# Gate matrices of a product-key expert layer: one-hot matrices built for eight tokens by two wide VectorE instructions, and gate matmuls that write the four tokens of a PSUM bank interleaved

## The chip, the cores and the metric

One Trainium2 chip, one core of it. The metric is the device time of one execution of the whole kernel in microseconds (us). The median of three runs of the kernel before is 1547.26 us (1546.43 to 1547.27).

## The reference, cut to what matters

The kernel computes two transformer-like blocks over 256 tokens of width 1024. The part that the change touches is in the first block, the PEER layer: per token and head (8 heads) it finds the 16 best of 128 x 128 product keys and weights those experts by a softmax.

```python
def peer(h, w_query, sub_keys, u_tab, v_tab):
    ...
    fv, fpos = lax.top_k(cand, P_TOPK)                 # 16 per head, 8 heads: 128 slots per token
    eidx = jnp.take_along_axis(cidx, fpos, axis=-1)    # expert = i1 * 128 + i2
    g = jax.nn.softmax(fv, axis=-1)
    u = u_tab[eidx]
    act = gelu(einsum('td,thkd->thk', xb, u))
    return einsum('thk,thkd->td', g * act, v_tab[eidx])
```

The kernel gathers nothing. It computes the activations of all 16384 experts densely (`peer_u`, 128 units of 128 experts), multiplies them by a gate that is zero where a token did not choose an expert, and multiplies the product by `peer_v`. The gate of one token is a 128 x 128 matrix: entry (i2, i1) is the sum of the weights g of the slots that chose that expert. With the 128 slots on the partitions it is one matmul of two one-hot matrices, one of them scaled by g.

## The kernel before, in words

`peer` has three stages that matter here. **Search** (lines 795 to 926) finds the experts, and `finish` leaves, for each slot (partition) and token, the two indices `ib[:, 0]` and `ib[:, 1]` and the weight. The weight is scaled by 32768 and split in two terms that are exact in fp16, `gp[:, 0]` and `gp[:, 1]`; all four are fp32 rows of 256 tokens. **Gate stage** (lines 928 to 965) builds the gate matrices. **Product stage** (from line 967) multiplies and streams `peer_v`.

The gate stage runs 32 groups of eight tokens (`OG` = 8). For a group, `onehots` issues on VectorE, per token, one `tensor_scalar` that compares a row 0..127 (`iob`, fp16) with the token's second index (`o`, line 941), and two that compare it with the first index and multiply by one half of the weight (`go`, line 943): 24 instructions of 128 elements. The loop calls `onehots(og + 1)` ahead of the matmuls of group og; `o` and `go` have two buffers. TensorE then does, per token, two accumulating matmuls of 128 columns, `o` stationary and `go` moving (line 958): 16 per group, four tokens side by side in each of two PSUM banks. ScalarE scales each bank into the staging tile `stg` (line 961), laid out as index, then 16 tokens, so that what it writes is one fp32 word in every 64 bytes. Every second group ScalarE's queue issues a 1 MB store of `stg` to the DRAM tensor `gd` (line 963).

Behind the gate matmuls of each group the loop puts one unit of `peer_u`, `U`: `fill` (lines 101 to 122) issues a 1 MB load on SP's queue for two units, casts one later unit on ScalarE (`whi`, line 112) and subtracts for another on VectorE (`wlo`, line 120), three to four units ahead of use; 24 matmuls of 256 columns follow (lines 163 to 165), then a Gelu on ScalarE (line 793). Order on each engine is program order. On VectorE a group is therefore 24 one-hot instructions and one `wlo`; on TensorE 16 gate matmuls and 24 matmuls of the unit; on ScalarE two `stg`, one `whi`, one Gelu.

Before the stage TensorE runs units alone, the last of them ending where the first gate matmul starts. Behind it seven units are left (`UKEEP`), and the product stage loads `gd` back (`gload`, line 979) once its last store has landed.

Of the kernel before, what the change touches and what calls it, by code (L numbers as in the profile page):

```python
# [13 lines left out]
F32 = mybir.dt.float32  # L14
F32R = mybir.dt.float32r
BF = mybir.dt.bfloat16
F16 = mybir.dt.float16
# [3 lines left out]
OP = mybir.AluOpType  # L21
# [4 lines left out]
T = 256  # L26
# [9 lines left out]
UKEEP = 7  # L36
TG = 16
OG = 8
GI = 8
LOADS = 9  # L40
SPLITS = 4
GSCALE = 32768.0
# [22 lines left out]
class Kx:  # L65
# [696 lines left out]
    def peer(self):  # L762
        nc, tc, a = self.nc, self.tc, self.a
# [4 lines left out]
        drp = ctx.enter_context(tc.tile_pool(name="pdr", bufs=1, space=DRAM))  # L768
        c1 = ExitStack()
        pz = c1.enter_context(tc.tile_pool(name="pz", bufs=1))  # L770
        gp = pz.tile([128, 2, T], F32, name="gp")
        ib = pz.tile([128, 2, T], F32, name="ib")
        acts = {}
        c2 = ExitStack()
        pk = c2.enter_context(tc.tile_pool(name="pk", bufs=1))
# [20 lines left out]
        with c2:  # L796
# [39 lines left out]
            for hd in range(1, 8):  # L836
# [5 lines left out]
                for i in range(2 if hd > 1 else 0):  # L842
                    p = self.unit("w_query", 2 * hd + i, h)
# [11 lines left out]
            pf_ = c2.enter_context(tc.tile_pool(name="pf", bufs=1))  # L855
# [4 lines left out]
            def finish():  # L860
                g = [pf_.tile([128, 8, 16], F32, name=f"g{tt}") for tt in range(2)]
                pf = [pf_.tile([128, 2, 8, 16], F32, name=f"pf{tt}") for tt in range(2)]
                sxf = [pf_.tile([128, 2, 8, 16], F32, name=f"sxf{tt}") for tt in range(2)]
                for tt in range(2):
                    v = fv[tt]
                    nc.vector.tensor_tensor(g[tt], v, v[:, :, 0:1].to_broadcast([128, 8, 16]), op=OP.subtract)
                    nc.scalar.activation(g[tt], g[tt], AF.Exp)
                for tt in range(2):
                    pi = pft.tile([128, 2, 8, 16], U32, name="pi")
                    nc.vector.tensor_scalar(pi[:, 0], fx[tt], 4, None, op0=OP.logical_shift_right)  # L870
                    nc.vector.tensor_scalar(pi[:, 1], fx[tt], 15, None, op0=OP.bitwise_and)
                    nc.vector.tensor_copy(sxf[tt].rearrange("p s h a -> p h s a"), sx[tt])
                    nc.vector.tensor_copy(pf[tt], pi)
                for tt in range(2):
                    gz = pft.tile([128, 8], F32, name="gz")
                    nc.vector.tensor_reduce(gz, g[tt], axis=AX.X, op=OP.add)
                    nc.vector.reciprocal(gz, gz)
                    nc.vector.tensor_tensor(g[tt], g[tt], gz[:, :, None].to_broadcast([128, 8, 16]), op=OP.mult)
                for _ in range(FW):
                    yield  # L880
                for tt in range(2):
                    p = self.side()
                    for j, src in enumerate((sxf[tt][:, 0], sxf[tt][:, 1], pf[tt][:, 0], pf[tt][:, 1])):
                        nc.tensor.transpose(p[:, j * 128:(j + 1) * 128], src.rearrange("p a b -> p (a b)"),
                                            self.ident)
                    ts = slice(tt * 128, (tt + 1) * 128)
                    p = p.rearrange("p (k s t) -> p k s t", k=2, s=2)
                    nc.scalar.copy(sxT[:, :, ts], p[:, 0])
                    nc.scalar.copy(posT[:, :, ts], p[:, 1])
                p = self.side()  # L890
                for tt in range(2):
                    nc.tensor.transpose(p[:, tt * 128:(tt + 1) * 128], g[tt].rearrange("p a b -> p (a b)"),
                                        self.ident)
                slot = pf_.tile([128, T], F32, name="slot")
                nc.scalar.mul(slot, p[:, :T], GSCALE)
                yield
                acc = self.bank(0)
                last = None
                for a0 in range(0, 16, FA):
                    cur = []  # L900
                    for a in range(a0, a0 + FA):
                        pb = self.side()
                        nc.tensor.matmul(pb, pick[:, a].rearrange("p h w -> p (h w)"),
                                         sxT.rearrange("p s t -> p (s t)"), start=True, stop=True)
                        t = pft.tile([128, 2 * T], BF, name="hit", bufs=2 * FA)
                        nc.vector.scalar_tensor_tensor(t, posT.rearrange("p s t -> p (s t)"), float(a), pb,
                                                       op0=OP.is_equal, op1=OP.mult)
                        cur.append((a, t))
                    yield
                    for a, t in cur:  # L910
                        nc.tensor.matmul(acc, identb, t, start=a == 0, stop=a == 15)
                nc.scalar.copy(ib, acc.rearrange("p (j t) -> p j t", j=2))
                g16 = pf_.tile([128, T], F16, name="g16")
                nc.vector.tensor_copy(g16, slot)
                nc.vector.tensor_copy(gp[:, 0], g16)
                nc.vector.tensor_tensor(gp[:, 1], slot, gp[:, 0], op=OP.subtract)

            self.side_cycle = ("s", "s", "a1", "a2")
            self.tasks.append(finish())
            while self.tasks:  # L920
                self.tick()
                if len(pre) > T // OG + UKEEP:
                    U(pre.popleft())
            while len(pre) > T // OG + UKEEP:
                U(pre.popleft())
            self.side_cycle = ("s",)

        with ExitStack() as c3:
            pg = c3.enter_context(tc.tile_pool(name="pg", bufs=1))
            pgt = c3.enter_context(tc.tile_pool(name="pgt", bufs=2))  # L930
            iob = pg.tile([128, 128], F16, name="iob")
            nc.gpsimd.iota(iob, pattern=[[1, 128]], base=0, channel_multiplier=0,
                           allow_small_or_imprecise_dtypes=True)
            stg = None

            def onehots(og):
                o = pgt.tile([128, OG, 128], F16, name="o")
                go = pgt.tile([128, OG, 2, 128], F16, name="go")
                for i in range(OG):
                    t = slice(og * OG + i, og * OG + i + 1)  # L940
                    nc.vector.tensor_scalar(o[:, i], iob, ib[:, 1, t], None, op0=OP.is_equal)  # L941
                    for j in range(2):
                        nc.vector.tensor_scalar(go[:, i, j], iob, ib[:, 0, t], gp[:, j, t],  # L943
                                                op0=OP.is_equal, op1=OP.mult)
                return o, go

            nxt = onehots(0)
            for og in range(T // OG):
                o2, go = nxt
                if og + 1 < T // OG:  # L950
                    nxt = onehots(og + 1)
                if og % (TG // OG) == 0:
                    stg = pgt.tile([128, 128, TG], F32, name="stg")
                for q in range(OG // 4):
                    p = self.side().rearrange("p (t i) -> p t i", t=4)
                    for i in range(4):
                        for j in range(2):
                            nc.tensor.matmul(p[:, i], o2[:, q * 4 + i], go[:, q * 4 + i, j],  # L958
                                             start=i == 0 and j == 0, stop=j == 1, skip_group_check=True)
                    e0 = (og % (TG // OG)) * OG + q * 4  # L960
                    nc.scalar.mul(stg[:, :, e0:e0 + 4].rearrange("p i t -> p t i"), p, 1.0 / GSCALE)
                if og % (TG // OG) == TG // OG - 1:
                    nc.scalar.dma_start(gd[:, og * OG // TG], stg)
                if len(pre) > UKEEP:
                    U(pre.popleft())
# [3 lines left out]
        with ExitStack() as c4:  # L969
# [5 lines left out]
            def gload(i):  # L975
                if i * GI < NB:
                    gts[i] = gt = pv.tile([128, 8 * (T + 2)], F32, name="gt")[:, :8 * T].rearrange(
                        "p (g e) -> p g e", g=T // TG)
                    (nc.gpsimd if i < 2 else nc.scalar).dma_start(gt, gd[:, :, i * GI:(i + 1) * GI].rearrange("p g i t -> p g (i t)"))

            wts = {}

            def w_mult(b):
                if b >= NB:
                    return
                t = acts[b]
                gv = gts[b // GI][:, :, (b % GI) * TG:(b % GI + 1) * TG]
                tv = t.rearrange("p (g t) -> p g t", t=TG)
                nc.vector.tensor_tensor(tv, tv, gv, op=OP.mult)  # L989
                if b % GI == GI - 1:  # L990
                    gload(b // GI + 2)

# [583 lines left out]
```

## Time and profile before

| | us |
|---|---|
| median of three runs | 1547.26 |
| the profiled execution | 1546.58 |
| its span in the trace | 1544.9 |
| first one-hot instruction | 379.89 |
| first matmul of the first unit in the gate stage | 384.93 |
| first matmul of the last unit in the gate stage | 570.04 |

Times in the views below count from the span's start. A row of a group of instructions gives the count, the busy time in us, the mean duration of one in ns, and the idle time of the engine ahead of them with what ended it. A duration contains the start-up that overlaps with the instruction before, so the pace of a row of instructions is read from start to start.

### The profile page before, as it was taken

To read this page: it belongs to the slowest core of one execution; us is meant where nothing else is said; L and a number is where in the kernel's file an instruction comes from. 1 tells how busy PE (TensorE), PEld (TensorE's weight loads), DVE (VectorE), ACT (ScalarE), POOL (GpSimd) and SP (SyncE) were. 2 spreads that over 40 slices of the span, in tenths; PEclk is the share of its full clock that TensorE was granted. 3 is DMA by queue.
4 is the path that set the end of the run, shared out by engine and by line. 5 is a ranking of instruction groups with operands and counts; after the bars stand their busy time and mean duration, and the time that the engine had idled before them with its cause. 6 is when DMAs were issued, how large, how long until landed. Compare 5 with 4: busy or idle time off the path is not lost.

```text
span 1544.9 us, 28187 instructions
## 1 busy us (share of the span) xinstructions
PE 1427.4 (92%) x11206; PEld 1351.2 (87%) x11208; DVE 1204.3 (78%) x2723; ACT 765.9 (50%) x1225; POOL 240.9 (16%) x143
## 2 busy tenths in 40 slices
PE   3897888979998999999999999999989989999997
PEld 2777777978777779999999999999989979989997
DVE  7887789997999996777777776666689968775554
ACT  3445554434555555544444454454564485554443
POOL 1443253310000000000000000000057740310000
PEclk8898989989999999999999999999999999999999
DMA  9365543434444458888888887677534434435642
GB/s 377 141 239 181 191 150 136 154 122 162 161 167 186 169 206 308 297 307 312 303 308 286 294 285 233 219 244 241 179 114 163 164 109 164 164 138 190 205 165 81
DMA packets 106068, 317.36 MB, mean 205 GB/s; under 512 B 5584, under 2 KB 34640, under 8 KB 103632
## 3 DMA queue, kind: packets, MB, share of 16 engines
q1 hardware_dynamic: 65696, 250.54, 45.8%
q10 hardware_dynamic: 39408, 61.87, 11.4%
q0 software_dynamic: 832, 3.15, 0.6%
q8 instruction: 88, 1.44, 0.4%
q14 instruction: 44, 0.36, 0.1%
HBM read 297.71 MB, written 17.83 MB: 204 GB/s over the span
## 4 chain that ended last, share of the span: by engine, by line
PE 56%; DVE 34%; ACT 4%; DMA 3%; issue 2%; POOL 1%; DVEq 0%; SPq 0%; ACTq 0%; POOLq 0%
PE a L163 10%; PE a L164 10%; PE a L165 10%; PE m L163 8%; PE m L164 8%; PE m L165 8%; DVE go L943 7%; DVE wlo L120 5%; DVE a L1138 3%; DVE o L941 3%; DVE junk L326 2%; DMA mraw<-in_ada_w 1%; ACT whi L112 1%; DMA raw<-in_ada_w 1%; DVE mdt L294 1%
## 5 line engine op out<-in xcount | busy, mean ns | idle before, releaser
L163 PE MATMUL m<-hi,whi 128*128 128x256 f32 x1816 | 526.5, 290 | 9.2 <-DVE cacc L556 6.0
L165 PE MATMUL m<-hi,wlo 128*128 128x256 f32 x1816 | 516.9, 285 | 9.4 <-DVE wlo L120 9.4
L164 PE MATMUL m<-lo,whi 128*128 128x256 f32 x1816 | 517.0, 285 | 0.0
L112 ACT CAST whi<-raw 128x1024 fp32r<-128x1024 f32 x428 | 444.6, 1046 | 50.1 <-DMA raw<-in_peer_v 19.5
L120 DVE TENSOR_TENSOR wlo<-raw,whi 128x1024 fp32r<-128x1024 f32 x350 | 437.7, 1269 | 30.9 <-ACT whi L112 23.0
L163 PEld LDWEIGHTS m<-hi,whi 128*128 128x128 f32 x1816 | 352.1, 194 | 16.1 <-issue 5.4
L165 PEld LDWEIGHTS m<-hi,wlo 128*128 128x128 f32 x1816 | 351.1, 193 | 10.7 <-DVE wlo L120 10.4
L164 PEld LDWEIGHTS m<-lo,whi 128*128 128x128 f32 x1816 | 351.7, 194 | 0.6
L165 PE MATMUL a<-wh,wlo 128*128 128x256 f32 x1024 | 288.2, 281 | 0.0
L164 PE MATMUL a<-wl,whi 128*128 128x256 f32 x1024 | 288.2, 281 | 0.0
L163 PE MATMUL a<-wh,whi 128*128 128x256 f32 x1024 | 287.9, 281 | 0.0
L120 POOL TENSOR_TENSOR wlo<-raw,whi 128x1024 fp32r<-128x1024 f32 x81 | 202.2, 2510 | 223.0 <-ACT whi L112 196.1
L165 PEld LDWEIGHTS a<-wh,wlo 128*128 128x128 f32 x1024 | 192.9, 188 | 0.0
L164 PEld LDWEIGHTS a<-wl,whi 128*128 128x128 f32 x1024 | 192.7, 188 | 0.0
L163 PEld LDWEIGHTS a<-wh,whi 128*128 128x128 f32 x1024 | 192.7, 188 | 0.0
L1001 DVE TENSOR_TENSOR wl<-act,wh 128x256 fp32r<-128x256 f32 x128 | 54.5, 426 | 140.5 <-PE a L164 125.7
L793 ACT ACTIVATE act<-m 128x256 f32<-128x256 f32 x126 | 48.5, 385 | 197.6 <-PE m L165 197.4
L943 DVE TENSOR_SCALAR go<-iob,ib,gp 128x128 f16<-128x128 f16 x512 | 138.8, 319 | 0.0
L996 ACT CAST wh<-act 128x256 fp32r<-128x256 f32 x128 | 51.9, 406 | 141.7 <-DVE act L989 118.8
L326 DVE SCALAR_TENSOR_TENSOR junk<-mraw,silu 128x1024 bf16<-128x1024 f32 x80 | 104.2, 1303 | 6.3 <-DMA mraw<-in_ada_w 6.0
L220 POOL TENSOR_TENSOR act<-act 128x256 f32<-128x256 f32 x7 | 5.6, 800 | 548.7 <-ACT act L211 548.3
L958 PE MATMUL s<-go,o 128*128 128x128 f16 x512 | 74.1, 219 | 18.3 <-DVE go L943 17.5
(438 smaller groups left out, 1962.0 us busy)
## 6 DMA issues: line engine op xcount, KB each, us to landing
raw<-in_peer_u SPq DMA_DIRECT2D x64, 1024.0 KB, 5.8
raw<-in_peer_v SPq DMA_DIRECT2D x64, 1024.0 KB, 5.3
mraw<-in_w_ada ACTq DMA_DIRECT2D x48, 512.0 KB, 5.8
raw<-in_w_ffn_in SPq DMA_DIRECT2D x22, 1024.0 KB, 5.1
gd<-stg ACTq DMA_DIRECT2D x16, 1024.0 KB, 3.9
gt<-gd ACTq DMA_DIRECT2D x14, 1024.0 KB, 8.7
mraw<-in_ada_w SPq DMA_DIRECT2D x24, 512.0 KB, 3.8
raw<-in_w_ffn_out SPq DMA_DIRECT2D x11, 1024.0 KB, 5.0
```

The costliest lines, as they stand in the source:

```text
L112: self.nc.scalar.copy(t, self.raw[k])
L120: eng.tensor_tensor(t, self.raw.pop(k), h.bitcast(F32), op=OP.subtract)
L163: mm(out, w[0], x[0], start=start, stop=False, **kw)
L164: mm(out, w[0], x[1], start=False, stop=False, **kw)
L165: mm(out, w[1], x[0], start=False, stop=stop, **kw)
L326: self.nc.vector.scalar_tensor_tensor(junk, w, 0.5, self.silu_c[i], op0=OP.mult, op1=OP.mult, accum_out=self.mod[i][:, u:u + 1])
L793: nc.scalar.activation(t, p, AF.Gelu)
L941: nc.vector.tensor_scalar(o[:, i], iob, ib[:, 1, t], None, op0=OP.is_equal)
L943: nc.vector.tensor_scalar(go[:, i, j], iob, ib[:, 0, t], gp[:, j, t], op0=OP.is_equal, op1=OP.mult)
L958: nc.tensor.matmul(p[:, i], o2[:, q * 4 + i], go[:, q * 4 + i, j], start=i == 0 and j == 0, stop=j == 1, skip_group_check=True)
L996: nc.scalar.copy(wts[b], acts[b])
L1001: nc.vector.tensor_tensor(wl, acts.pop(b), wts[b].bitcast(F32), op=OP.subtract)
```

## The change

`ib` and `gp` become one fp16 tile `ig` [128, 2, T, 2], with the two indices of a token side by side, and the two halves of its weight. `finish` writes them there; one copy (line 914 or 915) goes. A new function `spread` copies, on ScalarE, the values of 16 tokens eight times over into `rep` (two buffers), once per two groups and one block of 16 ahead. `onehots` now issues two `tensor_tensor` instructions of 2048 elements per group: one compares all 16 index values of eight tokens with the row 0..127, giving both one-hot matrices of each token (`o`, now with both); the other multiplies the first-index matrices by the two halves of the weight (`go`). Their innermost runs are eight fp16 values that lie next to each other, read again 16 times along the row. The gate matmuls write every fourth word of the bank, so that the four tokens of an index lie together, and `stg` copies runs of four words.

```diff
-        gp = pz.tile([128, 2, T], F32, name="gp")
-        ib = pz.tile([128, 2, T], F32, name="ib")
+        ig = pz.tile([128, 2, T, 2], F16, name="ig")
+        ib, gp = ig[:, 0], ig[:, 1]
...
-                nc.scalar.copy(ib, acc.rearrange("p (j t) -> p j t", j=2))
-                g16 = pf_.tile([128, T], F16, name="g16")
-                nc.vector.tensor_copy(g16, slot)
-                nc.vector.tensor_copy(gp[:, 0], g16)
-                nc.vector.tensor_tensor(gp[:, 1], slot, gp[:, 0], op=OP.subtract)
+                nc.scalar.copy(ib.rearrange("p t j -> p j t"), acc.rearrange("p (j t) -> p j t", j=2))
+                nc.vector.tensor_copy(gp[:, :, 0], slot)
+                nc.vector.tensor_tensor(gp[:, :, 1], slot, gp[:, :, 0], op=OP.subtract)
...
+            rep = {}
+            def spread(c):
+                if c < T // RC:
+                    sh = [128, 2, RC * 2, RW]
+                    rep[c] = t = pgt.tile(sh, F16, name="rep")
+                    s = ig[:, :, c * RC:(c + 1) * RC].rearrange("p k t j -> p k (t j)")
+                    nc.scalar.copy(t, s[:, :, :, None].to_broadcast(sh))
+
             def onehots(og):
-                o = pgt.tile([128, OG, 128], F16, name="o")
+                c, r = divmod(og * OG, RC)
+                if r == 0:
+                    spread(c + 1)
+                sh = [128, 2 * OG, 128 // RW, RW]
+                i8, g8 = [rep[c][:, k, 2 * r:2 * (r + OG)][:, :, None, :].to_broadcast(sh) for k in range(2)]
+                o = pgt.tile([128, OG, 2, 128], F16, name="o")
                 go = pgt.tile([128, OG, 2, 128], F16, name="go")
-                for i in range(OG):
-                    t = slice(og * OG + i, og * OG + i + 1)
-                    nc.vector.tensor_scalar(o[:, i], iob, ib[:, 1, t], None, op0=OP.is_equal)
-                    for j in range(2):
-                        nc.vector.tensor_scalar(go[:, i, j], iob, ib[:, 0, t], gp[:, j, t],
-                                                op0=OP.is_equal, op1=OP.mult)
-                return o, go
+                v = lambda x: x.rearrange("p t j (a b) -> p (t j) a b", b=RW)
+                io = iob[:, None, :].to_broadcast([128, 2 * OG, 128]).rearrange("p t (a b) -> p t a b", b=RW)
+                nc.vector.tensor_tensor(v(o), i8, io, op=OP.is_equal)
+                nc.vector.tensor_tensor(go.rearrange("p t j (a b) -> p t j a b", b=RW),
+                                        o[:, :, 0:1].to_broadcast([128, OG, 2, 128]).rearrange("p t j (a b) -> p t j a b", b=RW),
+                                        g8.rearrange("p (t j) a b -> p t j a b", j=2), op=OP.mult)
+                return o[:, :, 1], go
+
+            spread(0)
...
-                    p = self.side().rearrange("p (t i) -> p t i", t=4)
+                    p = self.side().rearrange("p (i t) -> p i t", t=4)
...
-                            nc.tensor.matmul(p[:, i], o2[:, q * 4 + i], go[:, q * 4 + i, j],
+                            nc.tensor.matmul(p[:, :, i], o2[:, q * 4 + i], go[:, q * 4 + i, j],
...
-                    nc.scalar.mul(stg[:, :, e0:e0 + 4].rearrange("p i t -> p t i"), p, 1.0 / GSCALE)
+                    nc.scalar.mul(stg[:, :, e0:e0 + 4], p, 1.0 / GSCALE)
```

`RC` is 16 and `RW` is 8.

## Rows read from the trace of the kernel before

**Rows 1.** The page's first part: busy time and share of the span by engine.

```profile
span 1544.9 us, 28187 instructions
PE 1427.4 (92%) x11206; PEld 1351.2 (87%) x11208; DVE 1204.3 (78%) x2723; ACT 765.9 (50%) x1225; POOL 240.9 (16%) x143
```

**Rows 2.** Busy time by stretch: before, in and behind the gate stage.

```profile
core 0: us, PE busy (x) PEld busy (x) DVE busy (x) ACT busy (x) POOL busy (x), PEclk, DMA share, GB/s
360.00:380.00 20.00, 19.95 (x161) 18.68 (x161) 12.61 (x16) 8.52 (x13) 0.24 (x1) 1.00 0.47 168
386.00:566.00 180.00, 162.75 (x1209) 132.11 (x1209) 180.00 (x751) 104.93 (x122) 0.00 (x0) 0.93 0.46 170
586.00:606.00 20.00, 20.00 (x172) 20.00 (x171) 14.25 (x21) 11.74 (x19) 0.00 (x0) 1.00 0.77 270
```

**Rows 3.** Groups of instructions by line and shape, 386 to 566 us.

```profile
L943 DVE TENSOR_SCALAR go<-iob,ib,gp 128x128 f16<-128x128 f16 x481 | 130.6, 320 | 0.0
L958 PE MATMUL s<-go,o 128*128 128x128 f16 x480 | 69.7, 219 | 17.2 <-DVE go L943 16.5
L961 ACT ACTIVATE stg<-s 128x512 f32<-128x512 f32 x61 | 65.0, 1066 | 40.2 <-PE s L958 38.8
L941 DVE TENSOR_SCALAR o<-iob,ib 128x128 f16<-128x128 f16 x240 | 62.2, 259 | 0.0
L120 DVE TENSOR_TENSOR wlo<-raw,whi 128x1024 fp32r<-128x1024 f32 x30 | 36.9, 1229 | 0.0
```

**Rows 4.** The chain that ended last, 386 to 398 us: shares, then start, us, what.

```profile
by line: DVE go L943 61.0%; DVE o L941 21.0%; DVE wlo L120 18.9%; issue 1.2%
389.73 1.13 DVE wlo L120
...
395.74 1.13 DVE wlo L120
```

**Rows 5.** TensorE in order of time: the stage's start, and its last unit's start.

```profile
382.38 0.28 PE L165 MATMUL m<-hi,wlo 128*128 128x256 f32 x1
382.85 0.71 PEld L958 LDWEIGHTS <-o 128*128 128x128 f16 x12
384.93 0.36 PE L163 MATMUL m<-hi,whi 128*128 128x256 f32 x1
570.04 0.37 PE L163 MATMUL m<-hi,whi 128*128 128x256 f32 x1
```

**Rows 6.** ScalarE and VectorE in order of time at the stage's start.

```profile
377.39 0.39 ACT L793 ACTIVATE act<-m 128x256 f32<-128x256 f32 x1 [1.51 <-PE m L165]
380.22 0.39 ACT L793 ACTIVATE act<-m 128x256 f32<-128x256 f32 x1 [1.51 <-PE m L165]
383.05 0.39 ACT L793 ACTIVATE act<-m 128x256 f32<-128x256 f32 x1 [1.51 <-PE m L165]
379.89 0.25 DVE L941 TENSOR_SCALAR o<-iob,ib 128x128 f16<-128x128 f16 x1
```

**Rows 7.** VectorE groups of the whole span: one-source casts and a two-source fp32 form.

```profile
L110 DVE CAST whi<-raw 128x1024 fp32r<-128x1024 f32 x3 | 2.1, 685 | 0.0
L915 DVE CAST gp<-g 128x256 f32<-128x256 f16 x1 | 0.3, 293 | 0.0
L989 DVE TENSOR_TENSOR act<-act,gt 128x256 f32<-128x256 f32 x128 | 53.6, 419 | 4.3 <-DMA gt<-gd 4.3
```

**Rows 8.** ScalarE groups of the whole span: contiguous copies and casts.

```profile
L112 ACT CAST whi<-raw 128x1024 fp32r<-128x1024 f32 x428 | 444.6, 1046 | 50.1 <-DMA raw<-in_peer_v 19.5 <-PE a L164 10.0 <-DVE go L943 6.8
L996 ACT CAST wh<-act 128x256 fp32r<-128x256 f32 x128 | 51.9, 406 | 141.7 <-DVE act L989 118.8 <-DVE junk L326 11.0 <-issue 6.9
L912 ACT COPY ib<-a 128x512 f32<-128x512 f32 x1 | 0.6, 589 | 0.5 <-PE a L911 0.5
```

**Rows 9.** DMA issues: engine, count, KB each, median us from issue to landing.

```profile
raw<-in_peer_u SPq DMA_DIRECT2D x64, 1024.0 KB, 5.8
gd<-stg ACTq DMA_DIRECT2D x16, 1024.0 KB, 3.9
```

More of the change, by code (lines that the diff above doesn't have):

```diff
@@ L38 @@
 OG = 8
+RC = 16
+RW = 8
 GI = 8
```

## The prediction

> **What bounds the kernel now.** I read the page's busy shares first, then the stretches, because a share of the span says nothing of one stage. Over the span TensorE is busy 92% and VectorE 78% [rows 1]. By stretch it turns round: ahead of the gate stage and behind it TensorE is busy 19.95 and 20.00 of 20 us, while from 386 to 566 VectorE is busy 180.00 of 180 and TensorE 162.75 at a granted clock of 0.93 [rows 2]. In this stage alone VectorE is the bound. The groups of instructions say with what: 130.6 us of `go`, 62.2 of `o`, 36.9 of `wlo`, all with no idle time ahead of them, while the gate matmuls sat idle waiting for `go` [rows 3]. The chain that ended last runs through these three and nothing else: 61.0% + 21.0% + 18.9% [rows 4].
>
> The period of a group is read from one `wlo` to the next, 395.74 - 389.73 = 6.01 us, of which 1.13 is the `wlo` [rows 4] and 4.88 the 24 one-hot instructions. From the first unit's first matmul at 384.93 to the last unit's at 570.04 [rows 5] there are 31 periods: 185.1 us. Behind that point nothing in the code changes, so what the change is worth is how much earlier the last unit starts. Sums are made against the profiled execution, 1546.58 us, 1.7 over its span and 0.7 under the median; I add 0.7 at the end.
>
> **VectorE, the part that the change is about.** The 24 instructions become two of 2048 elements. The trace has no two-source instruction on 2-byte data, so its rate lies between two rows. Two fp32 sources go at (1229 - 419) / 768 = 1.05 ns per element [rows 3, 7]; a cast with one fp32 source at (685 - 293) / 768 = 0.51 ns [rows 7]. Both take in 4 bytes per 0.51 to 0.53 ns. Two fp16 sources are 4 bytes per element, as in the cast, so I take its rate: half the price of two fp32 sources. From start to start a `wlo` of 1024 elements takes 1.13 us [rows 4], so 2048 elements cost 1.13 us at this rate, and 1.13 + 1.07 = 2.20 at the single rate. VectorE's group becomes 2 x 1.13 + 1.13 = **3.39 us**, at worst 2 x 2.20 + 1.13 = **5.53**, against 6.01. That the runs are short (eight values, read 16 times over) I price at nothing; if each restart cost, it would go towards the 5.53.
>
> [...]
>
> **TensorE, the next bound.** A unit alone takes 380.22 - 377.39 = 2.83 us, Gelu to Gelu [rows 6]. Four of its matmuls of 256 columns take 382.85 - 382.38 = 0.47 [rows 5], so 128 columns take 0.059, and the weight loads of the gate matmuls keep that pace: (0.71 - 0.10) / 11 = 0.056 [rows 5]. The 16 gate matmuls of a group cost 0.94 when nothing holds them. The change lets them write every fourth word of the bank. No matmul in the trace writes with gaps, so this is bounded from both sides. Below: 0.059 each; less is excluded, since as many columns go through. Above, from the only row that writes single words with gaps, `stg`: 512 words take 1066 ns [rows 3], against 589 for 512 words side by side [rows 8]. ScalarE's slope for contiguous words is (1046 - 406) / 768 = 0.83 ns [rows 8], which leaves 0.16 us of fixed time and 1.76 ns per word with gaps; 128 words at that are 0.23 us. Of what lies between I take the ratio of the two ScalarE rows, 1066 / 589 = 1.81, on the matmul's own 0.059: 0.107 each. It is the only evidence on gaps, and a ratio carries over to another engine better than a duration. Then 16 x 0.107 = 1.71, and a group on TensorE takes 2.83 + 1.71 = **4.54 us**; with free gaps 2.83 + 0.94 = **3.77**; at the upper end 2.83 + 3.68 = **6.51**.
>
> [...]
>
> **ScalarE and the queues.** `stg` now writes four words side by side: between 0.59 [rows 8] and 1.07 [rows 3] each, I take 0.6. `spread` adds 512 values per two groups, about 0.62 us between 406 ns for 256 and 1046 for 1024 [rows 8], so 0.31 a group. With `whi` 1.05 and Gelu 0.39 [rows 6, 8] a group is 2 x 0.6 + 0.31 + 1.44 = 2.95, at worst 3.9: covered by TensorE's 4.54, and just uncovered at 3.77. The transfers per group (0.5 MB of `peer_u`, 0.5 MB of `gd`) now fall in 4.54 us instead of 6.01: 230 GB/s, or 277 in 3.77. Behind the stage 270 GB/s ran beside a TensorE busy throughout [rows 2], and a load lands in 5.8 us [rows 9] against three buffers of two units each. Priced at nothing. In `finish` a copy of 293 ns [rows 7] goes and `ib` may take up to 0.48 more on ScalarE (gaps, as for `stg`); the units run three ahead, so I take nothing.
>
> **The start is a cost.** Now the first one-hots start at 379.89, while TensorE is still on the unit before [rows 6]. `spread(0)` is issued behind that unit's Gelu, which starts at 383.05 and takes 0.39 [rows 6]; ScalarE is first in, first out. So `spread(0)` ends near 384.0, the two wide instructions near 385.2 and 386.4, and the first gate matmul starts at about 386.45 instead of 382.85 [rows 5]. TensorE idles 3.6 us there, once. The first unit starts at 386.45 + 1.71 = 388.16, 3.2 later than now.
>
> **The sum.** 388.16 + 31 x 4.54 = 528.9 against 570.04: 41.1 us earlier. 1546.58 - 41.1 = 1505.5, and against the median **1506**.
>
> **The rivals.**
> - *Free gaps.* 386.45 + 0.94 + 31 x 3.77 = 504.3, 65.8 earlier: **1481**. For it: a matmul may have room on its way out that ScalarE has not. Against: the one row with gaps pays 1.81 times. VectorE (3.39) and ScalarE (2.95) would be close behind.
> - *The wide instructions don't widen.* At the single rate VectorE stays the bound at 5.53. From 384.05 (`spread(0)` plus a hand-over) 32 pairs of 4.40 and 31 `wlo` of 1.13 end at 559.9, the last gate matmuls 0.9 later: 560.8, 9.2 earlier, **1538**. For it: every two-source row runs at 1.05 ns. Against: the bytes per ns of the casts.
> - *Slower: matmuls with gaps at ScalarE's pace.* At 0.23 each the last unit starts at 386.45 + 3.68 + 31 x 6.51 = 591.9, 21.9 later: **1569**. It decides from the point where 386.45 + 16c + 31 x (2.83 + 16c) reaches 570.04, c = 0.187, 3.2 times the present price. For it: TensorE is what is late next, so every ns of a gate matmul counts 512 times. Against: it needs the absolute rate of a slower engine.
>
> **How the numbers follow.** Forecast 0.40, free gaps 0.32, no widening 0.10, slower 0.10; 0.03 for other gains, 0.04 for no change (a wait not seen here that eats it), 0.01 for other losses. A measurement of this kernel can tell about 0.2%, 3 us, from no change. Faster 0.85, same 0.04, slower 0.11. The range holds the three faster cases, 1478 to 1541, 0.85 of the chance. The forecast's own range, with a gate matmul at 0.095 to 0.12 (6 us each way), is 1500 to 1513.
>
> **What would show it.** Right: VectorE's two instructions per group at some 1.2 us each and VectorE no longer busy throughout; gate matmuls in rows of 16 at 0.107 from start to start; TensorE busy without idle time at a period of 4.5, and one gap near 383 to 386. Wrong: a period of 3.8 (free gaps); VectorE busy throughout at 5.5 with instructions of 2.2 us; gate matmuls above 0.187; TensorE idle behind ScalarE or a load, which none of the cases has.

## The result, and the profile after

The changed kernel takes 1509.39 us (median, 1508.18 to 1511.66) against 1547.15 for the kernel before, run beside it: a ratio of 0.976 (95% interval 0.974 to 0.978), 37.8 us less. The forecast was 1506, 41 us less. The profiled execution of the changed kernel is the longest of its four, 1511.66 us with a span of 1510.0; against the profiled span of before it is 34.9 us shorter.

The gate stage after, groups of instructions by line and shape from 395 to 520 us (to be held against [rows 3]):

```profile
L974 PE MATMUL s<-go,o 128*128 128x128 f16 x434 | 52.3, 312 | 0.0
...
L956 DVE TENSOR_TENSOR go<-o,rep 128x2048 f16<-128x2048 f16 x28 | 34.3, 1225 | 1.0
L122 DVE TENSOR_TENSOR wlo<-raw,whi 128x1024 fp32r<-128x1024 f32 x28 | 34.1, 1217 | 0.0
L955 DVE TENSOR_TENSOR o<-rep,iob 128x2048 f16<-128x2048 f16 x27 | 33.1, 1225 | 26.2 <-PE s L974 26.2
L977 ACT ACTIVATE stg<-s 128x512 f32<-128x512 f32 x54 | 32.3, 598 | 14.1 <-PE s L974 14.0
```

The 24 one-hot instructions of a group are two of 1.22 us. The waiting has turned round: before, TensorE waited for `go`; now VectorE sat idle 26.2 us waiting for the gate matmuls, and these waited for nothing. The mean gate matmul went from 219 to 312 ns, the staging copy from 1066 to 598.

The chain that ended last in the changed kernel, 400 to 425 us (start, us, what); before, this was VectorE alone [rows 4]:

```profile
by line: PE s L974 40.5%; PE m L167 20.4%; PE m L166 19.7%; PE m L165 19.6%
...
400.76 1.76 PE s L974 x16
...
405.35 1.76 PE s L974 x16
...
409.93 1.76 PE s L974 x16
```

It is TensorE and nothing else. The period is 405.35 - 400.76 = 4.59 us, and 16 gate matmuls take 1.76, which is 0.110 each from start to start; a bank without gaps was priced at 0.94. The start of the stage, TensorE, VectorE and ScalarE in the changed kernel [rows 5, 6]:

```profile
386.02 0.28 PE L167 MATMUL m<-hi,wlo 128*128 128x256 f32 x1
386.34 0.38 ACT L795 ACTIVATE act<-m 128x256 f32<-128x256 f32 x1 [1.51 <-PE m L167]
386.62 1.12 ACT L943 COPY rep<-ig 128x512 f16<-128x512 f16 x2
387.33 1.22 DVE L955 TENSOR_TENSOR o<-rep,iob 128x2048 f16<-128x2048 f16 x1 [4.07 <-ACT rep L943]
388.59 1.23 DVE L956 TENSOR_TENSOR go<-o,rep 128x2048 f16<-128x2048 f16 x1
389.87 2.50 PE L974 MATMUL s<-go,o 128*128 128x128 f16 x16 [3.56 <-DVE go L956]
392.01 0.56 PE L165 MATMUL m<-hi,whi 128*128 128x256 f32 x1
```

Gelu, `spread`, the two wide instructions and the first gate matmul follow one another as the prediction laid them out, and TensorE idles 3.56 us. VectorE a little later in the stage, in order of time, one group from `wlo` to `wlo`:

```profile
392.12 1.22 DVE L122 TENSOR_TENSOR wlo<-raw,whi 128x1024 fp32r<-128x1024 f32 x1
393.26 1.22 DVE L955 TENSOR_TENSOR o<-rep,iob 128x2048 f16<-128x2048 f16 x1
394.51 1.23 DVE L956 TENSOR_TENSOR go<-o,rep 128x2048 f16<-128x2048 f16 x1
395.65 1.22 DVE L122 TENSOR_TENSOR wlo<-raw,whi 128x1024 fp32r<-128x1024 f32 x1
```

Busy time by stretch, from the idle time on (the column after POOL is the granted clock, as a share of full speed):

```profile
386.20:389.80 3.60, 0.10 (x1) 0.10 (x1) 2.44 (x3) 1.41 (x3) 0.00 (x0) 1.00 0.41 165
389.90:393.30 3.40, 3.40 (x22) 3.40 (x22) 3.37 (x4) 1.50 (x3) 0.00 (x0) 0.67 0.00 0
393.50:396.90 3.40, 3.40 (x28) 3.36 (x28) 3.34 (x3) 1.12 (x3) 0.00 (x0) 0.86 0.00 0
```

The granted clock was 1.00 from 360 to 386 us; behind the idle time it was 0.67 from 389.9 to 393.3 and 0.86 from 393.5 to 396.9.

### The profile page after: what moved, and what is told of

It reads as the page before. It is cut to its first block, busy times and chain, and to the rows that moved or that the text cites. A ratio compares the mean times of both kernels' runs of the same rounds, so it can differ in the third digit from the quotient of the medians.

```text
span 1510.0 us, 27484 instructions
## 1 busy us (share of the span) xinstructions
PE 1408.5 (93%) x11206; PEld 1362.8 (90%) x11208; DVE 1126.9 (75%) x2018; ACT 745.4 (49%) x1241; POOL 240.8 (16%) x143
## 4 chain that ended last, share of the span: by engine, by line
PE 67%; DVE 24%; ACT 4%; DMA 2%; issue 2%; POOL 1%; DVEq 0%; SPq 0%; ACTq 0%; POOLq 0%
PE m L165 10%; PE m L166 10%; PE m L167 10%; PE a L165 10%; PE a L166 10%; PE a L167 10%; PE s L974 4%; DVE wlo L122 3%; DVE a L1154 3%; DVE junk L328 2%; DMA mraw<-in_ada_w 1%; DMA raw<-in_ada_w 1%; DVE mdt L296 1%; DVE lo L303 1%; ACT whi L114 1%
## 5 line engine op out<-in xcount | busy, mean ns | idle before, releaser
L167 PEld LDWEIGHTS m<-hi,wlo 128*128 128x128 f32 x1816 | 347.2, 191 | 10.8 <-DVE wlo L122 10.5
L166 PEld LDWEIGHTS m<-lo,whi 128*128 128x128 f32 x1816 | 347.8, 192 | 0.7
L974 PE MATMUL s<-go,o 128*128 128x128 f16 x512 | 62.0, 314 | 3.6 <-DVE go L956 3.6
L955 DVE TENSOR_TENSOR o<-rep,iob 128x2048 f16<-128x2048 f16 x32 | 39.2, 1225 | 32.2 <-PE s L974 28.2
```

Source lines behind the costliest of these rows:

```text
L166: mm(out, w[0], x[1], start=False, stop=False, **kw)
L167: mm(out, w[1], x[0], start=False, stop=stop, **kw)
L955: nc.vector.tensor_tensor(v(o), i8, io, op=OP.is_equal)
L974: nc.tensor.matmul(p[:, :, i], o2[:, q * 4 + i], go[:, q * 4 + i, j], start=i == 0 and j == 0, stop=j == 1, skip_group_check=True)
```

## The experiments

Three things were to be settled: that the dear gate matmuls come from the gaps and not from their operands; that the double rate of VectorE comes from the runs of eight and not from the type alone; and what the idle time at the start is worth. Seven kernels were run, each beside runs of the kernel before on the same chip; ratios are to these. The medians of the kernel before lie between 1546.58 and 1547.25 us, so that medians of different runs can be held against each other too.

**The bank written without gaps.** The changed kernel, with gate matmuls and staging copy as they were:

```diff
-                    p = self.side().rearrange("p (i t) -> p i t", t=4)
+                    p = self.side().rearrange("p (t i) -> p t i", t=4)
...
-                            nc.tensor.matmul(p[:, :, i], o2[:, q * 4 + i], go[:, q * 4 + i, j],
+                            nc.tensor.matmul(p[:, i], o2[:, q * 4 + i], go[:, q * 4 + i, j],
...
-                    nc.scalar.mul(stg[:, :, e0:e0 + 4], p, 1.0 / GSCALE)
+                    nc.scalar.mul(stg[:, :, e0:e0 + 4].rearrange("p i t -> p t i"), p, 1.0 / GSCALE)
```

> The changed kernel, with the gate matmuls writing 128 words side by side again and ScalarE writing single words with gaps again. Theory (the gaps make the gate matmul dear): from start to start a gate matmul falls from 0.110 to 0.059 us, TensorE needs 2.83 + 0.94 = 3.77 us a group; the staging copy goes back from 0.60 to 1.07 and ScalarE becomes the bound at 2 x 1.07 + 1.05 + 0.38 + 0.30 + 0.17 = 4.04; 31 periods of 4.04 instead of 4.59 make about 1492 us. Rival (the price comes from the operands: the stationary matrix now lies interleaved with another, or VectorE's wide writes take SBUF from TensorE): gate matmuls stay at 0.110, the period at 4.6 or above, 1509 or more.

Measured: 1486.99 us, ratio 0.961 (0.959 to 0.963). Groups from 400 to 515 us:

```profile
L977 ACT ACTIVATE stg<-s 128x512 f32<-128x512 f32 x60 | 60.5, 1118 | 6.4 <-DMA gd<-stg 6.4
...
L974 PE MATMUL s<-go,o 128*128 128x128 f16 x464 | 31.2, 220 | 1.6 <-ACT stg L977 1.6
```

The same run in order of time, gate matmuls and one pair of staging copies:

```profile
443.93 1.07 PE L974 MATMUL s<-go,o 128*128 128x128 f16 x16
447.72 1.07 PE L974 MATMUL s<-go,o 128*128 128x128 f16 x16
451.51 1.07 PE L974 MATMUL s<-go,o 128*128 128x128 f16 x16
...
446.12 2.01 ACT L977 ACTIVATE stg<-s 128x512 f32<-128x512 f32 x2 [1.25 <-DMA gd<-stg]
```

Same operands, no gaps, and the gate matmul is back at 220 ns; the period is 451.51 - 447.72 = 3.79. The gaps are the price. The theory's second half missed: at 3.79 the period is TensorE's own (3.77 forecast), not ScalarE's 4.04. The theory's sum took durations, but two staging copies in a row take 2.01 us from the first start to the last end, not 2 x 1.12, and the other copies overlap likewise (a `whi` of 1.07 us starts at 447.91, the Gelu behind it at 448.87).

ScalarE and its stores are close behind, though. `stg` waited 6.4 us for a `gd` store to land, for `stg` has two buffers, and the chain that ended last from 440 to 452 us runs through store and ScalarE. The profiled execution is the longest of its four, 1494.61 us against 1482.94 to 1488.08, and shows a cost behind the stage: the last store lands 8.2 us after its issue, VectorE then waits 10.5 us for the load that brings `gd` back (3.8 in the changed kernel), and TensorE idles 4.0 us for a Gelu that stands behind this work on ScalarE. Chain from 505 to 545 us, two pieces, and TensorE in order of time:

```profile
513.17 8.22 DMA gd<-stg
522.15 11.06 DMA gt<-gd
...
535.42 0.58 PE L165 MATMUL m<-hi,whi 128*128 128x256 f32 x1 [4.01 <-ACT act L795]
```

Whether the shorter executions escaped this is not shown; they left no trace.

**The gaps alone, in the kernel before.** The reverse of that edit, put into the kernel before.

> The kernel before, with only the interleaved bank: gate matmuls write every fourth word, the staging copy writes runs of four words. Theory: gate matmuls that wait for nothing run at 0.110 from start to start, the staging copy takes 0.60, and all of it is hidden under VectorE at a period of 6.0: within 3 us of 1547. Rival (operands): the gate matmuls stay at 0.059 here, as their operands are those of before; the time is the same by both, so the verdict is in the rows.

Measured: 1546.71 us, ratio 1.000 (0.999 to 1.001). From 400 to 515 us:

```profile
L958 PE MATMUL s<-go,o 128*128 128x128 f16 x308 | 57.9, 290 | 7.0
...
L961 ACT ACTIVATE stg<-s 128x512 f32<-128x512 f32 x39 | 23.3, 599 | 42.5 <-PE s L958 42.5
```

With the operands of before, the mean gate matmul goes from 219 to 290 ns and the staging copy from 1066 to 599, and neither moves the time: VectorE, busy 115.00 of 115 us, covers both. Many gate matmuls wait here, but those that don't start 0.11 us apart, as at 387.43, 387.54 and 387.65. That the price shows here too rules the operands out. The same edit costs nothing before and some 22 us after the widening.

**Step zero in place of the runs of eight.** The changed kernel without `spread`; index and weight are read from `ig` 128 times each:

```diff
-                if r == 0:
-                    spread(c + 1)
...
-                i8, g8 = [rep[c][:, k, 2 * r:2 * (r + OG)][:, :, None, :].to_broadcast(sh) for k in range(2)]
+                src = [ig[:, k, og * OG:(og + 1) * OG].rearrange("p t j -> p (t j)") for k in range(2)]
+                i8, g8 = [s[:, :, None, None].to_broadcast(sh) for s in src]
...
-            spread(0)
```

> The changed kernel without the copies that ScalarE makes: the two wide instructions read each index and weight 128 times with a step of zero. Theory (the double rate needs 2-byte values next to each other in every input): each wide instruction takes 2048 x 1.05 ns + 0.06 = 2.2 us, VectorE bounds the stage at about 2.2 + 2.3 + 1.13 = 5.6 a group, the start is a few us earlier: about 1540 us. Rival (the type alone gives the rate): 1.2 us each, period 4.59, about 1506.

Measured: 1541.97 us, ratio 0.997 (0.996 to 0.999). VectorE in order of time:

```profile
440.81 1.22 DVE L122 TENSOR_TENSOR wlo<-raw,whi 128x1024 fp32r<-128x1024 f32 x1
441.95 2.28 DVE L954 TENSOR_TENSOR o<-ig,iob 128x2048 f16<-128x2048 f16 x1
444.27 2.29 DVE L955 TENSOR_TENSOR go<-o,ig 128x2048 f16<-128x2048 f16 x1
446.48 1.22 DVE L122 TENSOR_TENSOR wlo<-raw,whi 128x1024 fp32r<-128x1024 f32 x1
```

2.28 us in place of 1.22, and a period of 446.48 - 440.81 = 5.67: with the same types and counts each of the two instructions ran at the single rate (2048 elements in 2.28 us, where an fp32 `wlo` takes 1.22 for 1024) when the innermost step of one input was zero. This is the rival without widening in real form; it was priced at 1538. So the type alone did not give the rate: 1.22 us with runs of eight, 2.28 with a step of zero.

**Pairs instead of fours.** The changed kernel with every second word written, 8 bytes apart instead of 16:

```diff
-                    p = self.side().rearrange("p (i t) -> p i t", t=4)
+                    p = self.side().rearrange("p (h i t) -> p h i t", h=2, t=2)
...
-                            nc.tensor.matmul(p[:, :, i], o2[:, q * 4 + i], go[:, q * 4 + i, j],
+                            nc.tensor.matmul(p[:, i // 2, :, i % 2], o2[:, q * 4 + i], go[:, q * 4 + i, j],
...
-                    nc.scalar.mul(stg[:, :, e0:e0 + 4], p, 1.0 / GSCALE)
+                    nc.scalar.mul(stg[:, :, e0:e0 + 4].rearrange("p i (h t) -> p h i t", h=2), p, 1.0 / GSCALE)
```

> The changed kernel with tokens interleaved in pairs: a gate matmul writes every second word, 8 bytes apart, the staging copy writes runs of two words. Theory A (any gap between words costs one full step per word): gate matmuls stay at 0.110, period 4.6, about 1509. Theory B (the price grows with the distance): 0.059 to 0.085, TensorE 3.8 to 4.2 a group, 1485 to 1497 if the staging copy stays near 0.6, at most 4.04 a group and 1492 if it goes back to 1.07.

Measured: 1508.84 us, ratio 0.976 (0.974 to 0.977), as the changed kernel. Groups from 400 to 515 us:

```profile
L974 PE MATMUL s<-go,o 128*128 128x128 f16 x403 | 48.5, 312 | 0.0
...
L977 ACT ACTIVATE stg<-s 128x512 f32<-128x512 f32 x50 | 31.1, 622 | 12.8 <-PE s L974 12.8
```

The chain that ended last, 440 to 452 us:

```profile
441.52 1.76 PE s L974 x16
446.10 1.76 PE s L974 x16
```

Theory A: 16 gate matmuls take the same 1.76 us at 8 bytes as at 16. Between these two distances the price does not grow. Against a bank without gaps it is a factor of about 1.9: 1.76 us for sixteen here and 0.91 without gaps in the next run. ScalarE's writes differ: runs of two words cost 622 ns, hardly more than runs of four (598).

**The gaps moved to ScalarE's read.** Gate matmuls write side by side, by the same two lines as in the bank written without gaps; the staging copy reads the bank with gaps and writes runs of four:

```diff
-                    nc.scalar.mul(stg[:, :, e0:e0 + 4], p, 1.0 / GSCALE)
+                    nc.scalar.mul(stg[:, :, e0:e0 + 4], p.rearrange("p t i -> p i t"), 1.0 / GSCALE)
```

> The changed kernel with the interleaving moved to ScalarE's read: gate matmuls write 128 words side by side, the staging copy reads PSUM with gaps and writes runs of four words. Theory A (a copy pays for gaps on the side that it writes only): staging copy 0.60, gate matmul 0.059, TensorE bounds the stage at 3.77 to 3.85 a group, 0.75 less than the changed kernel, about 1485, and the transfers (1 MB per group) are the next thing late. Theory B (gaps in what it reads cost the same as in what it writes): staging copy 1.07 as in the run with plain banks, 3.95 to 4.04 a group, 1487 to 1492.

Measured: 1486.64 us, ratio 0.961 (0.958 to 0.963). Groups from 400 to 500 us:

```profile
L974 PE MATMUL s<-go,o 128*128 128x128 f16 x427 | 28.5, 220 | 0.0
L977 ACT ACTIVATE stg<-s 128x512 f32<-128x512 f32 x52 | 28.3, 598 | 1.0
```

The chain, 440 to 456 us:

```profile
442.64 0.91 PE s L974 x16
446.44 0.91 PE s L974 x16
```

Theory A: 598 ns, the same as without gaps on either side, and 3.80 us a group. Here ScalarE paid for single words with gaps in what it wrote to SBUF (1118 ns in the plain bank), not in what it read from PSUM (598). That this is no faster than the plain bank (1486.64 and 1486.99) fits: TensorE bounds both at 3.8. In the traces this one is 2.1 us shorter from the first gate matmul to the last unit (119.98 against 122.06); in the plain bank's, TensorE waits 1.6 us for staging copies; the medians don't tell the two apart.

**The first copy on VectorE.** In the changed kernel, only `spread(0)` moves:

```diff
-                    nc.scalar.copy(t, s[:, :, :, None].to_broadcast(sh))
+                    (nc.scalar.copy if c else nc.vector.tensor_copy)(t, s[:, :, :, None].to_broadcast(sh))
```

> The changed kernel with the first copy of the index values (16 tokens) on VectorE instead of ScalarE; all later ones stay on ScalarE. Theory (the idle 3.6 us of TensorE at the start is the wait of that copy behind the Gelu of the unit before): the copy runs right behind VectorE's subtraction, the two wide instructions end about when the unit before does, TensorE's idle time falls to 0.5 or less, and with it the low clock of the groups behind it: 3 to 5.5 us less, 1504 to 1506. Rival (the start waits for something else, the memory of the stage before or the indices): no change in the idle time, 1509.

Measured: 1505.20 us (1502.89 to 1505.83), ratio 0.973 (0.971 to 0.975). VectorE and TensorE in order of time at the start, and the last unit's first matmul:

```profile
381.57 0.42 DVE L943 COPY rep<-ig 128x512 f16<-128x512 f16 x1
...
384.41 0.28 PE L167 MATMUL m<-hi,wlo 128*128 128x256 f32 x1
384.63 1.91 PE L974 MATMUL s<-go,o 128*128 128x128 f16 x16
...
528.59 0.36 PE L165 MATMUL m<-hi,whi 128*128 128x256 f32 x1
```

Busy time in the stretch behind it, granted clock after POOL:

```profile
386.00:390.00 4.00, 4.00 (x37) 3.96 (x36) 3.97 (x4) 2.44 (x5) 0.00 (x0) 1.00 0.02 6
```

TensorE goes from the last unit into the gate matmuls without idle time, the granted clock stays at 1.00 from 386 to 390 us, and the median is 4.2 us lower. In the traces, from the last matmul ahead of the stage to the last unit, it is 528.59 - 384.41 = 144.2 us against 535.29 - 386.02 = 149.3 in the changed kernel, 5.1 less. The idle time was the wait of the first copy, as the theory has it.

**Both.** Gaps in ScalarE's read, first copy on VectorE.

> Both edits together: interleaving in ScalarE's read, first copy on VectorE. If both theories hold, 3.77 to 3.85 a group and no idle time at the start: about 1480 to 1483; if the transfers of a faster stage are late, the part that they take shows as idle time of TensorE or of VectorE ahead of the subtraction: 1484 to 1490.

Measured: 1480.34 us (1476.99 to 1485.71), ratio 0.957 (0.954 to 0.960), the fastest of all: 29 us under the changed kernel, 67 under the one before. TensorE is busy 100.00 of 100 us in the stage; transfers run at a share of 0.84 and delay nothing that TensorE waits for there. Busy time by stretch:

```profile
400.00:500.00 100.00, 100.00 (x1061) 98.82 (x1059) 95.52 (x80) 70.27 (x119) 0.00 (x0) 1.00 0.84 277
```

## Why the prediction was right, point by point

The mechanism held: VectorE's bound lifted, TensorE the next one, and the gaps deciding what it costs. By its steps:

- **VectorE.** Forecast 3.39 us a group, from two instructions of 1.13. From start to start the first takes 1.25 and the second 1.14; the second reads what the first has just written and starts 0.03 us behind its end (394.51 against 394.48), where the `wlo`, which reads none of it, starts 0.09 ahead of the end before it (395.65 against 395.74). That hand-over was not in the sum. With the `wlo` it is 3.53, still under TensorE. The choice between the ends (bytes per ns, as in the casts) was right, and the run with a step of zero shows the other end at 5.67, forecast 5.53. The argument for the choice was thinner than it reads: one of the two casts behind the 0.51 ns has an fp16 source [rows 7], and the run with a step of zero has the same types and counts at about half the rate (2.28 us against 1.22), so bytes per ns alone don't decide. Pricing the short runs at nothing held: 1225 ns for 2048 elements in 256 runs, against 1217 for the `wlo`, whose pace the price was taken from.
- **The gate matmul with gaps.** Forecast 0.107 from the ratio of ScalarE's rows, measured 0.110. The number came out by luck more than by reason. On ScalarE the price hangs on the side and on the length of the run (598 ns reading with gaps, 622 writing pairs, 1066 writing single words); on TensorE pairs cost as much as fours (1.76 us for sixteen matmuls in both). The ratio of one engine's rows was an analogy that fell near the other's price, not a law behind both.
- **The period.** Forecast 4.54, measured 4.59: 0.05 for the gate matmuls, times 31.
- **ScalarE and the queues.** 598 ns for the staging copy, as taken. A store of `gd` went from 3.9 us [rows 9] to 6.4 from issue to landing, and nothing waited for it here. That was right for this kernel and would not have been for the plain bank, whose staging copies waited 6.4 us.
- **The start.** Forecast 3.6 us idle, measured 3.56; `spread(0)` starts behind that unit's Gelu (386.62 and 386.34), as laid out. What the step left out is the granted clock behind the idle time, 0.67 and then 0.86, where the run with the first copy on VectorE, without this idle time, has 1.00: the last of the first 16 gate matmuls and about the first eleven of the first unit's 24 matmuls ran slower. Matmuls of this unit start 0.21 us apart at its beginning (392.37, 392.58, 392.80), and 0.12 apart from 394.48 on. The first 16 took 392.01 - 389.87 = 2.14 us instead of 1.71. From the first unit's start to the last unit's it was 535.29 - 392.01 = 143.3 us, 1.0 more than 31 periods of 4.59: that is the first unit.
- **The sum.** In the trace the last unit starts at 535.29; forecast 528.9. Of the 6.4 us, 3.3 were there ahead of the stage, about 0.5 are the start and the first gate matmuls, 1.5 the period and 1.0 the first unit. The 3.3 are in this execution ahead of the first changed operation: the last unit's Gelu ahead of the stage starts at 386.34 against 383.05 [rows 6], and a Gelu early in the expert layer is already 3.2 late. The granted clock from 150 to 200 us was 0.84 there against 0.95 before, and in the traces of the seven kernels with the same code up to that point this Gelu starts between 235.46 and 240.92, so a difference of this size lies within the scatter. The other three terms, 3.0 together, are the real miss. The other executions are shorter than this one, and against the median the forecast is 3 us low.

That early Gelu in the kernel before, in order of time on ScalarE:

```profile
237.72 0.38 ACT L793 ACTIVATE act<-m 128x256 f32<-128x256 f32 x1
```

The same one and, on TensorE, the last unit's first matmul, in the changed kernel:

```profile
240.92 0.38 ACT L795 ACTIVATE act<-m 128x256 f32<-128x256 f32 x1 [0.87 <-PE m L167]
...
535.29 0.36 PE L165 MATMUL m<-hi,whi 128*128 128x256 f32 x1
```


The rivals: free gaps (1481) is near what the kernels without gaps in the matmuls reach, 1487, and 1480 with the start mended. No widening (1538) is the run with a step of zero, 1542. The slower case would have needed 0.187 us per gate matmul and got 0.110.

## What to carry to other kernels

When an engine's load is halved, price what the change puts on the next engine as if nothing covered it: the interleaved bank costs nothing under a bound VectorE (ratio 1.000) and some 22 us once TensorE is the bound. A layout has to be turned somewhere; look for the side that does it for nothing, here ScalarE's read of PSUM (598 ns with gaps and without), and keep gaps out of what TensorE writes (sixteen gate matmuls in 1.76 us with gaps, 0.91 without). At the seam of two stages, put the first hand-over on the engine that is idle there: 5.1 us in the traces, 4.2 by the medians, for one copy.

## What the runs showed of the hardware that was not expected

- A gate matmul of 128 columns that wrote words with gaps took 0.110 us from start to start, against 0.057 without gaps (1.76 and 0.91 for sixteen), and 8 bytes apart took as long as 16.
- ScalarE read 512 words of a PSUM bank at a step of 128 words in 598 ns, as without gaps; it wrote pairs of words in 622 ns and single words in 1066 to 1118.
- An input read with a step of zero took the two two-source fp16 instructions of VectorE from 1.22 to 2.28 us, with types and counts unchanged.
- Idle time of 3.56 us on TensorE was followed by a lower granted clock, here (0.67 from 389.9 to 393.3 us) and in the three other kernels with that idle time (0.65 in the plain bank from 392 to 395, 0.62 with pairs from 385 to 389, 0.50 with gaps in the read from 389 to 392); with the first copy on VectorE and no idle time it stayed at 1.00 from 386 to 390, and with both edits the first unit's matmuls started 0.12 us apart from 385.67 on.
